# Branch sums and the first norm's bias added by accumulating transfers

## The chip, the cores and the metric

The kernel runs on one core of one Trainium2 chip. Five engines work beside each other, each through its own list of instructions in order: TensorE (PE, with its weight loads PEld), VectorE (DVE), ScalarE (ACT), GpSimd (POOL) and SyncE (SP). They wait for each other through semaphores. Transfers are issued from SP's queue or from GpSimd's and are carried out by 16 DMA engines that the queues share. The metric is the time of one execution in microseconds of device time; less is better.

## What is computed

One layer of a hybrid decoder on 256 tokens of width 2048, all in float32. What the change touches are the merging of three mixer branches and the first norm:

```python
gates = jax.nn.sigmoid(gate_logits.reshape(bsz, seq, N_BRANCH, D_MODEL) + b_gate)
merged = (gates[:, :, 0] * (y_lru @ w_branch[0])
          + gates[:, :, 1] * (y_gla @ w_branch[1])
          + gates[:, :, 2] * (y_dn @ w_branch[2]))
return merged @ w_out
...
x = _layernorm(DEEPNORM_ALPHA * x + m, ln1_g[l], ln1_b[l])
h = _squared_relu_mlp(x, mlp_w1[l], mlp_b1[l], mlp_w2[l], mlp_b2[l])
x = _layernorm(DEEPNORM_ALPHA * x + h, ln2_g[l], ln2_b[l])
```

The norm is `(xf - mu) * rsqrt(var + eps) * g + b`.

## The kernel before

**Jobs.** The kernel is a row of jobs. Each job has 1 MB of weights (`raw`, three buffers), loaded on SP's queue. ScalarE copies them to a rounded high part `hi` (line 93) and VectorE subtracts that to get the low part `lo` (line 94), eight blocks of 128x128 at a time, with three buffers for each; then TensorE multiplies with three products (high by high, low by high, high by low). The function `run_jobs` loads and splits the weights of the next job ahead of the matmuls of this one.

**Side work.** What is not part of a job is written as Python generators in the list `live`. After each job, `pump` steps them; `yield None` ends a generator's turn until the next job has been written. So a step behind `yield None` stands in TensorE's list one job later.

**The branch sums.** For each branch b (0 to 2) and each block cb of 512 columns (0 to 3), four jobs give the gate logits (`accG`), which become `gate` tiles, and two jobs give the branch's projection (`accY`). `evac_branch` then takes each of the two token halves tt: VectorE forms the product (line 907); for b = 0 it is written to the sum `mg`, for b = 1 and 2 it is written over the gate tile `t` and GpSimd adds it to `mg` (line 908). When the last branch is added, `gen_merged` is put on the list: its first step allocates and yields None, its second has TensorE transpose `mg` in 128x128 pieces into `p_m` (line 922), one job later. The gate tiles come from a pool of eight buffers (`t2`).

**The first norm.** After the output projection the tiles `xt[tt, i]` (four of 128x1024) hold the first norm's input. The MLP is fed from a normalized copy. For the second residual, `gen_res` multiplies `xt` by the row g (line 1143), adds the row b (line 1145), then scales by alpha and adds the MLP's second bias (line 1150). It runs during the first MLP jobs (`accB`, 5.6 us each). The rows are loaded on GpSimd's queue, broadcast to 128 partitions, by `row` (line 1135); each row is two tiles of 128x1024 and each tile a transfer of 512 KB.

Of the kernel before, what the change touches and what calls it, by code (L numbers as in the profile page):

```python
# [11 lines left out]
ALU = mybir.AluOpType  # L12

P = 128
# [50 lines left out]
def trunk_kernel(ctx, tc, xw, xtok, par, lat, con, wab, wa2, wB, wV, wR, wZ, wG, wBr, wO, w1, w2, rows, bg, out):  # L65
    nc = tc.nc
    ve, sc, te, gp = nc.vector, nc.scalar, nc.tensor, nc.gpsimd
# [15 lines left out]
    def b4_tile(name, shape, dt=F32):  # L83
        return b4.tile(shape, dt, tag="b4", name=name)
# [4 lines left out]
    def t1_tile(name, shape, dt=F32):  # L89
        return sm.tile(shape, dt, tag="t1", name=name, bufs=7)  # L90
# [807 lines left out]
    def evac_branch(b, cb):  # L898
        def f(tt, acc):
            if b == 0 and cb % 2 == 0:  # L900
                mg[tt, cb // 2] = b4_tile(f"mg{tt}", [P, 1024])
            m = mg[tt, cb // 2][:, (cb % 2) * 512:(cb % 2) * 512 + 512]
            t = gates.pop(tt)
            if b == 0:
                ve.scalar_tensor_tensor(m, t, 1.0, acc, ALU.add, ALU.mult)
                return
            ve.scalar_tensor_tensor(t, t, 1.0, acc, ALU.add, ALU.mult)
            gp.tensor_tensor(m, m, t, ALU.add)
            if b == 2 and tt == NT - 1:
                live.append(gen_merged(cb))  # L910
        return f

    def gen_merged(cb):
        mh.append(b4_tile(f"mh{cb}", [P, 4, T], F32R))
        ml.append(b4_tile(f"ml{cb}", [P, 4, T], F32R))
        yield None
        for kp in range(2):
            p = mx_tile("p_m")
            for a in range(2):
                c = (cb % 2) * 512 + (2 * kp + a) * P  # L920
                for tt in range(NT):
                    te.transpose(p[:, a * T + tt * P:a * T + (tt + 1) * P], mg[tt, cb // 2][:, c:c + P], ident)
            pv = p.rearrange("p (a t) -> p a t", a=2)
            hi, lo = mh[cb][:, 2 * kp:2 * kp + 2, :], ml[cb][:, 2 * kp:2 * kp + 2, :]
            sc.copy(hi, pv)
            ve.tensor_tensor(lo, pv, hi.bitcast(F32), ALU.subtract)
            yield (.7, .7)


    xt = {}  # L930
# [163 lines left out]
    for q in range(4):  # L1094
# [6 lines left out]
        for kp in range(2):  # L1101
# [6 lines left out]
            for a in range(2):  # L1108
                k = 4 * q + 2 * kp + a
                t = t1_tile("x1t", [P, T])  # L1110
# [20 lines left out]
    def row(i, nm):  # L1131
        t = []
        for j in range(2):
            r = b4_tile(f"{nm}{j}", [P, 1024])
            nc.gpsimd.dma_start(r, rows[i:i + 1, j * 1024:(j + 1) * 1024].to_broadcast([P, 1024]))
            t.append(r)
        return t

    def gen_res():
        g, b = row(0, "r_g1"), row(1, "r_b1")  # L1140
        for tt in range(NT):
            for i in range(2):
                ve.tensor_tensor(xt[tt, i], xt[tt, i], g[i], ALU.mult)
                yield (1.1, 0)
                ve.tensor_tensor(xt[tt, i], xt[tt, i], b[i], ALU.add)
                yield (1.1, 0)
        b2 = row(2, "r_b2")
        for tt in range(NT):
            for i in range(2):
                ve.scalar_tensor_tensor(xt[tt, i], xt[tt, i], ALPHA, b2[i], ALU.mult, ALU.add)  # L1150
                yield (1.1, 0)

    live.append(gen_res())


# [204 lines left out]
```

## Time and profile before

| | us |
|---|---|
| median of 3 runs | 1700.43 (lowest 1698.84) |
| the profiled execution | 1700.21, its span 1698.4 |
| TensorE busy | 1675.7 (99%) |
| VectorE busy | 1107.6 (65%) |
| ScalarE busy | 852.9 (50%) |
| GpSimd busy | 75.8 (4%) |
| DMA, all queues | 322.52 MB, mean 190 GB/s |

A timeline row gives start and duration in us, then engine, line, operation, the tile written and the tiles read, how many instructions are merged into the row, and in brackets the idle time of the engine just before and what ended it. Matmul ends are modelled: a matmul of 512 columns is drawn 0.39 us long, but the next one starts 0.23 us after it. The trace numbers lines as the listing above.

### The profile page before, as it was taken

How to read it: one execution, taken by the hardware profiler on the slowest of the kernel's cores; microseconds unless marked ns; L12 is line 12 of the kernel's file. 1: busy time of each engine (PE TensorE's matmuls, PEld its weight loads, DVE VectorE, ACT ScalarE, POOL GpSimd, SP SyncE). 2: the span in 40 equal slices, each digit the busy share in tenths (PEclk: the TensorE clock that was granted, in tenths of full speed). 3: DMA queues.
4: the chain of work that ended last, by engine and by line, in shares of the span. 5: the costliest groups of instructions: out<-in, count | busy, mean ns of one | idle time of the engine just before them, and what ended most of it. 6: DMA issues, size and time to landing. Idle time of an engine off the chain costs nothing.

```text
span 1698.4 us, 21498 instructions
## 1 busy us (share of the span) xinstructions
PE 1675.7 (99%) x8414; PEld 1416.8 (83%) x8414; DVE 1107.6 (65%) x1479; ACT 852.9 (50%) x1127; POOL 75.8 (4%) x94
## 2 busy tenths in 40 slices
PE   8999999999999999999999999999999999999997
PEld 7888887888888887888888788888888888888885
DVE  7877457788775596665556687555555555565556
ACT  6776445797444443444444454444444444444442
POOL 0000000000220203010010000000000000000000
PEclk9999999999999999999999999999999999999999
DMA  8445554444564556455565826555555555555553
GB/s 315 155 176 186 188 198 147 149 174 173 190 220 155 163 197 192 148 194 198 207 230 194 322 101 234 177 196 187 185 199 177 195 195 187 190 209 199 196 188 112
DMA packets 50774, 322.52 MB, mean 190 GB/s; under 512 B 6560, under 2 KB 6944, under 8 KB 14192
## 3 DMA queue, kind: packets, MB, share of 16 engines
q1 hardware_dynamic: 47696, 314.30, 52.4%
q0 software_dynamic: 2976, 6.84, 1.5%
q8 instruction: 66, 1.08, 0.3%
q14 instruction: 36, 0.29, 0.1%
HBM read 318.22 MB, written 2.88 MB: 189 GB/s over the span
## 4 chain that ended last, share of the span: by engine, by line
PE 97%; ACT 1%; DVE 1%; DMA 0%; issue 0%; SPq 0%; DVEq 0%
PE accB L131 22%; PE accB L133 12%; PE accM L1218 7%; PE accM L1219 7%; PE accM L1217 7%; PE accG L479 5%; PE accG L480 5%; PE accG L478 5%; PE accY L479 3%; PE accY L478 3%; PE accY L480 3%; PE accO L954 2%; PE accO L955 2%; PE accO L953 2%; PE acc L201 1%; PE accZ L478 1%
## 5 line engine op out<-in xcount | busy, mean ns | idle before, releaser
L94 DVE TENSOR_TENSOR lo<-raw,hi 128x1024 fp32r<-128x1024 f32 (+2 forms) x582 | 703.1, 1211 | 510.8 <-ACT hi L93 497.4
L93 ACT CAST hi<-raw 128x1024 fp32r<-128x1024 f32 (+2 forms) x582 | 601.7, 1037 | 735.0 <-PE accB L131 225.0
L131 PE MATMUL accB<-xx,hi 128*128 128x512 f32 x1696 | 427.5, 394 | 1.8 <-ACT hi L93 1.8
L131 PEld LDWEIGHTS accB<-xx,hi 128*128 128x128 f32 x1696 | 305.9, 189 | 58.9 <-ACT hi L93 1.9
L133 PEld LDWEIGHTS accB<-xx,lo 128*128 128x128 f32 x1696 | 232.1, 191 | 17.0 <-DVE lo L94 0.4
L133 PE MATMUL accB<-xx,lo 128*128 128x256 f32 x1696 | 237.2, 283 | 0.0
L1217 PE MATMUL accM<-hi,hh 128*128 128x512 f32 x488 | 189.8, 389 | 0.0
L1218 PE MATMUL accM<-hi,hl 128*128 128x512 f32 x488 | 189.8, 389 | 0.0
L1219 PE MATMUL accM<-lo,hh 128*128 128x512 f32 x488 | 189.8, 389 | 0.0
L478 PE MATMUL accG<-hi,xx 128*128 128x512 f32 x384 | 150.9, 393 | 0.0
L479 PE MATMUL accG<-hi,xx 128*128 128x512 f32 x384 | 149.9, 390 | 0.0
L480 PE MATMUL accG<-lo,xx 128*128 128x512 f32 x384 | 149.8, 390 | 0.0
L1217 PEld LDWEIGHTS accM<-hi,hh 128*128 128x128 f32 x488 | 91.6, 188 | 19.1
L1218 PEld LDWEIGHTS accM<-hi,hl 128*128 128x128 f32 x488 | 91.6, 188 | 19.0
L1219 PEld LDWEIGHTS accM<-lo,hh 128*128 128x128 f32 x488 | 91.6, 188 | 18.9
L480 PEld LDWEIGHTS accG<-lo,xx 128*128 128x128 f32 x384 | 72.1, 188 | 15.1
L479 PEld LDWEIGHTS accG<-hi,xx 128*128 128x128 f32 x384 | 72.1, 188 | 14.5
L478 PEld LDWEIGHTS accG<-hi,xx 128*128 128x128 f32 x384 | 72.1, 188 | 14.4
L478 PE MATMUL accY<-hi,yh 128*128 128x512 f32 x192 | 74.9, 390 | 0.0
L479 PE MATMUL accY<-hi,yl 128*128 128x512 f32 x192 | 74.7, 389 | 0.0
L480 PE MATMUL accY<-lo,yh 128*128 128x512 f32 x192 | 74.7, 389 | 0.0
L953 PE MATMUL accO<-hi,mh 128*128 128x512 f32 x128 | 49.9, 390 | 0.0
(322 smaller groups left out, 1758.4 us busy)
## 6 DMA issues: line engine op xcount, KB each, us to landing
raw<-in_w_dram SPq DMA_DIRECT2D x128, 1024.0 KB, 4.7
raw<-in_wG_dram SPq DMA_DIRECT2D x48, 1024.0 KB, 4.8
raw<-in_wB_dram SPq DMA_DIRECT2D x45, 1024.0 KB, 4.7
raw<-in_wBr_dram SPq DMA_DIRECT2D x24, 1024.0 KB, 4.8
raw<-in_wO_dram SPq DMA_DIRECT2D x16, 1024.0 KB, 4.8
raw<-in_wV_dram SPq DMA_DIRECT2D x8, 1024.0 KB, 4.7
raw<-in_wR_dram SPq DMA_DIRECT2D x8, 1024.0 KB, 4.7
raw<-in_wZ_dram SPq DMA_DIRECT2D x8, 1024.0 KB, 4.8
```

The lines of the kernel that those rows point to most:

```text
L93: i1 = sc.copy(hi, raw)
L94: i2 = ve.tensor_tensor(lo, raw, hi.bitcast(F32), ALU.subtract)
L131: te.matmul(acc, lhsT=hi[:, k, :], rhs=flat(r[:, k]), start=start and k == 0, stop=False)
L133: te.matmul(acc[:, :T], lhsT=lo[:, k, :], rhs=r[:, k, 0, :], start=False, stop=stop and k == 7)
L478: te.matmul(accs[tt], lhsT=sh, rhs=hi, start=k == 0, stop=False)
L479: te.matmul(accs[tt], lhsT=sl, rhs=hi, start=False, stop=False)
L480: te.matmul(accs[tt], lhsT=sh, rhs=lo, start=False, stop=k == 4 * nkg - 1)
L953: te.matmul(t, lhsT=sh, rhs=hi, start=k == 0, stop=False)
L954: te.matmul(t, lhsT=sl, rhs=hi, start=False, stop=False)
L1217: te.matmul(t, lhsT=sh, rhs=hi, start=k == 0, stop=False)
L1218: te.matmul(t, lhsT=sl, rhs=hi, start=False, stop=False)
L1219: te.matmul(t, lhsT=sh, rhs=lo, start=False, stop=k == NK2 - 1 and b % 512 == 0)
```

## The change

In `evac_branch` the GpSimd addition becomes a transfer that reads the product `t` and accumulates it into `mg`. In `gen_res` the row b is no longer loaded to two tiles, and the four VectorE additions become four transfers that read the row in DRAM, broadcast to 128 partitions, and accumulate it into `xt`; each is followed by `yield None`.

```diff
@@ -905,7 +905,7 @@
             ve.scalar_tensor_tensor(t, t, 1.0, acc, ALU.add, ALU.mult)
-            gp.tensor_tensor(m, m, t, ALU.add)
+            gp.dma_start(m, t, accum_op=ALU.add)
             if b == 2 and tt == NT - 1:
                 live.append(gen_merged(cb))
@@ -1137,13 +1137,13 @@
     def gen_res():
-        g, b = row(0, "r_g1"), row(1, "r_b1")
+        g = row(0, "r_g1")
         for tt in range(NT):
             for i in range(2):
                 ve.tensor_tensor(xt[tt, i], xt[tt, i], g[i], ALU.mult)
                 yield (1.1, 0)
-                ve.tensor_tensor(xt[tt, i], xt[tt, i], b[i], ALU.add)
-                yield (1.1, 0)
+                gp.dma_start(xt[tt, i], rows[1:2, i * 1024:(i + 1) * 1024].to_broadcast([P, 1024]), accum_op=ALU.add)
+                yield None
         b2 = row(2, "r_b2")
```

TensorE's list is the same; what changes there are waits. This is the first of the four places where a block of the merged sum is transposed (`mg` is the sum, a number for each token half, `p_m` the PSUM tile; a semaphore named Pool counts GpSimd's instructions, DMASW counts transfers of its queue):

```order
 L480 MATMUL accG<-lo,xx_75 128x512
-L922 MATMUL p_m<-ct,mg_4031 128x128 [waits PE_49,Pool_49]
-L922 MATMUL p_m<-ct,mg_4033 128x128 [waits Pool_49]
+L922 MATMUL p_m<-ct,mg_4031 128x128 [waits DMASW0_49,PE_49]
+L922 MATMUL p_m<-ct,mg_4033 128x128 [waits DMASW1_49]
 L922 MATMUL p_m<-ct,mg_4031 128x128
 L922 MATMUL p_m<-ct,mg_4033 128x128
```

The two transposes that read a token half first now wait for that half's transfer instead of GpSimd's addition; the other three places change in the same way.

This is the end of GpSimd's list, where the rows of the norms are loaded and the four tiles `xt_7360` to `xt_7367` get their bias (`r_b` stands for the tiles of the MLP's second bias, and before the change also of the norm's):

```order
 L1135 DMA r_g_8264<-in_rows_dram 128x1024
 L1135 DMA r_g_8266<-in_rows_dram 128x1024
-L1135 DMA r_b_8268<-in_rows_dram 128x1024
-L1135 DMA r_b_8270<-in_rows_dram 128x1024
-L1135 DMA r_b_8469<-in_rows_dram 128x1024
-L1135 DMA r_b_8471<-in_rows_dram 128x1024
...
+L1145 DMA xt_7360<-in_rows_dram 128x1024
+L1145 DMA xt_7362<-in_rows_dram 128x1024
+L1145 DMA xt_7365<-in_rows_dram 128x1024
+L1135 DMA r_b_8465<-in_rows_dram 128x1024
+L1145 DMA xt_7367<-in_rows_dram 128x1024
+L1135 DMA r_b_8467<-in_rows_dram 128x1024
```

The two loads of the MLP's second bias now stand behind the third and the fourth accumulating transfer, each of which waits for VectorE's product on its tile.

This is VectorE's list at the same place, of the changed kernel, from the second product to the last line 1150:

```order
L1143 TENSOR_TENSOR xt_7362<-xt_7362,r_g_8266 128x1024
L94 TENSOR_TENSOR lo<-raw,hi 128x1024
L1143 TENSOR_TENSOR xt_7365<-xt_7365,r_g_8264 128x1024
L1064 TENSOR_TENSOR hr<-accB,hr 128x256
L94 TENSOR_TENSOR lo<-raw,hi 128x1024
...
L1143 TENSOR_TENSOR xt_7367<-xt_7367,r_g_8266 128x1024
...
L1150 SCALAR_TENSOR_TENSOR xt_7360<-xt_7360,r_b_8465 128x1024
...
L1150 SCALAR_TENSOR_TENSOR xt_7362<-xt_7362,r_b_8467 128x1024
L1150 SCALAR_TENSOR_TENSOR xt_7365<-xt_7365,r_b_8465 128x1024
...
L1150 SCALAR_TENSOR_TENSOR xt_7367<-xt_7367,r_b_8467 128x1024
```

The four additions of line 1145 are gone from it, the products have moved closer together, and each line 1150 now waits for a transfer into its own tile as well as for the bias.

## Rows read from the trace of the kernel before

**Rows 1.** Busy part of the page: engine, us (share of the span) x instructions

```profile
PE 1675.7 (99%) x8414; PEld 1416.8 (83%) x8414; DVE 1107.6 (65%) x1479; ACT 852.9 (50%) x1127; POOL 75.8 (4%) x94
```

**Rows 2.** Chain that ended last, share of the span by engine

```profile
PE 97%; ACT 1%; DVE 1%; DMA 0%; issue 0%; SPq 0%; DVEq 0%
```

**Rows 3.** Waits of TensorE, all but the shortest: total us, times, longest us

```profile
PE acc L201 <- ACT hi L93: 4.9, 2, 4.2
PE p_x L1106 <- issue: 2.1, 1, 2.1
PE accB L131 <- ACT hi L93: 1.8, 1, 1.8
PE p_i L759 <- DVE q L752: 1.0, 1, 1.0
PE p_x L1106 <- DVE xt L1098: 0.6, 1, 0.6
```

**Rows 4.** Line 908: durations ns (min/median/max), first and last start us

```profile
L908 POOL TENSOR_TENSOR mg<-mg,gate x16: 1262/1298/2410, 636.8 to 886.5; 128x512 f32<-128x512 f32 x16
```

**Rows 5.** Timeline of 850 to 860 us, the rows of the merged sum

```profile
850.84 1.37 DVE L907 SCALAR_TENSOR_TENSOR gate<-gate,accY 128x512 f32<-128x512 f32 x2
...
851.67 3.53 POOL L908 TENSOR_TENSOR mg<-mg,gate 128x512 f32<-128x512 f32 x2 [30.01 <-DVE gate L907]
...
856.53 1.02 PEld L922 LDWEIGHTS p_m<-ct,mg 128*128 128x128 f32 x8
```

**Rows 6.** Line 922: durations ns, first and last start us

```profile
L922 PEld LDWEIGHTS p_m<-ct,mg x32: 138/140/142, 789.5 to 890.9; 128*128 128x128 f32 x32
```

**Rows 7.** DMA issues by line: KB each, median us from issue to landing

```profile
raw<-in_wG_dram SPq DMA_DIRECT2D x48, 1024.0 KB, 4.8
...
bgrow<-in_bg_dram SPq DMA_DIRECT2D x12, 256.0 KB, 4.2
...
out_dram<-xt SPq DMA_DIRECT2D x8, 256.0 KB, 2.1
wab<-in_wab_dram SPq DMA_DIRECT2D x2, 512.0 KB, 11.7
```

**Rows 8.** The same, stretches from 1022, 1029 and 962.5 us, GpSimd's queue

```profile
r_g<-in_rows_dram POOLq DMA_DIRECT2D x1, 512.0 KB, 3.6
...
r_g<-in_rows_dram POOLq DMA_DIRECT2D x1, 512.0 KB, 4.4
...
r_b<-in_rows_dram POOLq DMA_DIRECT2D x2, 512.0 KB, 8.3
```

**Rows 9.** Stretches: each engine's busy us, PEclk (granted clock), DMA share, GB/s

```profile
970.00:980.00 10.00, 6.99 (x39) 5.18 (x39) 7.54 (x21) 5.75 (x12) 0.54 (x1) 1.00 0.52 202
...
1684.00:1698.00 14.00, 2.42 (x11) 1.69 (x9) 10.28 (x20) 0.29 (x1) 0.00 (x0) 0.76 0.35 133
```

**Rows 10.** Lines 833 and 893: durations ns, first and last start us

```profile
L833 DVE TENSOR_TENSOR vn<-p_tv,btok x4: 681/682/684, 536.0 to 694.6; 128x512 f32<-128x512 f32 x4
...
L893 DVE TENSOR_TENSOR gate<-accG,bgrow x24: 671/692/693, 432.4 to 874.2; 128x512 f32<-128x512 f32 x24
```

**Rows 11.** VectorE's groups of 1000 to 1035 us: busy us, mean ns

```profile
L1145 DVE TENSOR_TENSOR xt<-xt,r_b 128x1024 f32<-128x1024 f32 x4 | 4.9, 1216 | 0.0
```

**Rows 12.** Timeline of VectorE from 968 us, three rows

```profile
1002.34 1.22 DVE L1143 TENSOR_TENSOR xt<-xt,r_g 128x1024 f32<-128x1024 f32 x1
...
1005.39 1.22 DVE L1143 TENSOR_TENSOR xt<-xt,r_g 128x1024 f32<-128x1024 f32 x1
...
1011.01 2.35 DVE L94 TENSOR_TENSOR lo<-raw,hi 128x1024 fp32r<-128x1024 f32 x2
```

**Rows 13.** Timeline of TensorE of 1009 to 1024 us, two rows

```profile
1016.84 2.00 PE L131 MATMUL accB<-xx,hi 128*128 128x512 f32 x8
1018.68 1.12 PE L133 MATMUL accB<-xx,lo 128*128 128x256 f32 x8
```

**Rows 14.** Line 1135: durations ns of an issue, first and last start us

```profile
L1135 POOL DMA_DIRECT2D r_b<-in_rows_dram x4: 537/537/538, 962.1 to 973.0; - x4
```

## The prediction

> **What bounds the kernel now.** Read the page's busy part first: TensorE is busy for 1675.7 of 1698.4 us, VectorE for two thirds of that, GpSimd for 75.8 us in all [rows 1]. Then the chain that ended last: 97% of it is TensorE [rows 2]. Then what TensorE waited for: the longest entries are 4.9 us at the start (`acc`) and a few around the first norm (`p_x`); neither `p_m` (line 922) nor any wait for GpSimd is in the list [rows 3]. So TensorE runs its list in order with hardly a gap, and an engine beside it matters only where TensorE has to stop for it. An edit that takes work from GpSimd and VectorE has little to give; the question is whether what replaces it makes TensorE stop.
>
> **The branch sums (line 908).** Removed are 16 GpSimd additions of 1.3 to 2.4 us [rows 4]. In the four places where a sum is complete, the rows show what hides them [rows 5]: VectorE writes both gate products (line 907) from 850.84 to 852.21, GpSimd adds them from 851.67 to 855.20, and TensorE starts the transposes (line 922) at 856.53, after one whole job of other matmuls. The additions end 1.3 us before TensorE comes to them. They cost nothing now, so removing them gives nothing.
>
> Added are 16 transfers of 256 KB that read two operands and write one. Eight of them (the second branch, b = 1) have the whole third branch's matmuls until anything reads the sum. Eight (b = 2) sit in four pairs, each one job ahead of its transposes, and TensorE's wait at line 922 is now on the two transfers. The time that the second transfer of a pair has: its product is ready at 852.21; GpSimd starts 0.14 us after a product is ready (850.84 + 0.69 = 851.53, start 851.67); so it is issued at 852.35. The transposes take turns between the two token halves, eight in 1.02 us, so the second sum is wanted at 856.53 + 0.13 = 856.66. That leaves 4.3 us from issue to landing. The other three places have the same spacing: the transposes' first and last starts are 789.5 and 890.9 [rows 6].
>
> No accumulating transfer is in the trace, so its landing is bounded by the nearest rows. From below: a 256 KB load in the same stage, beside the weight stream, but on SP's queue and with one operand, 4.2 us; a quiet 256 KB store 2.1 us [rows 7]. From GpSimd's own queue: 512 KB, as much as one such addition reads, landed in 3.6 us when it stood alone, in 4.4 us right after another, and in 8.3 us as the second of a pair [rows 8]. A pair of additions reads as much as that pair and writes half of it; a weight load of 1 MB, landing in 4.8 us [rows 7], goes on beside it in either case. I take the middle of 3.6 and 8.3 us, 5.9 us. TensorE then stops for 5.9 - 4.3 = 1.6 us at each of four places: 6.4 us. The bounds are 0 (anything that lands within 4.3 us) and 4 x (8.3 - 4.3) = 16 us. Nothing gives such a stop back: TensorE has no slack later in the run, its list is the same, and the engines that feed it only get further ahead. It costs no clock either: in the stretch 970 to 980 us TensorE was busy for 7.0 of 10 us and was granted 1.00; a mean of 0.76 shows only in the tail, with 2.4 of 14 us busy [rows 9].
>
> A rule speaks against this price. The Trainium skill, "DMA: Bandwidth & Descriptors", section "Anatomy of one DMA — SWDGE (gpsimd) path", fits a GpSimd-issued transfer at 2.0 us plus bytes over 436 GB/s. By it 256 KB land in an estimated 2.6 us and the sum would be 0. By the same fit 512 KB take an estimated 3.2 us; the trace has 3.6 us for one alone and 8.3 us in a pair [rows 8], so the fit holds here only without a neighbour, and the pairs of line 908 have one.
>
> The gate product is now held until its transfer has landed. Its buffer is one of eight that rotate; the next writers named in the order are line 833, last at 694.6 us, for the pair issued at 636 us, and line 893, at the next column block, some 33 us later (30.01 us of idle time and 3.53 us of additions) [rows 4, 5, 10]. Against any landing above that is free.
>
> **The norm's bias (line 1145).** Removed: four VectorE additions of 1.22 us, 4.9 us [rows 11], and two row loads. VectorE is full from 1002 to 1030 us but works ahead of TensorE: the low part that it finishes at 1011.01 + 2.35 = 1013.36 is first used at 1018.68, 5.3 us later [rows 12, 13]. So the 4.9 us are off the path too: no gain.
>
> Added: four transfers of 512 KB on GpSimd's queue, and in that queue the first load of the next bias stands behind the third of them, the second load behind the fourth. VectorE's line 1150 now waits for both. Working it through with VectorE's steps of 1.13 us (start to start) for a 128x1024 operation and 0.34 us for a 128x256 one: the second product starts at 1005.39 [rows 12], the third ends about 1008.8, so the first load is issued about 1009.5 (each issue takes 0.54 us [rows 14]); the fourth product ends about 1012.2 and the second load is issued about 1012.8. With 3.6 to 8.3 us they land at 1013.1 to 1017.8 and 1016.4 to 1021.1. VectorE comes to the two readers at about 1015.8 and 1018.3, so it stands still for 0 to 2.0 and 0 to 2.8 us, less than the 4.9 us taken from it and the 5.3 us of lead. Behind line 1150 stand the low parts (line 94) that TensorE wants, so more than about 10 us of standing still would reach it. Cost: 0, as long as the lead covers it.
>
> **The sum.** The profiled execution took 1700.2 us (span 1698.4 and 1.8 us around it), 0.2 us under the median shown. 1700.2 + 6.4 + 0 + 0.2 = 1706.8 us against that median.
>
> **The rivals.** (A) The transfers land within 4.3 us and are hidden: 1700 us, no change. For it: 3.6 and 4.2 us stand in the trace for as many or more bytes [rows 7, 8]. Against: those rows read one operand and have no twin issued half a microsecond before. The fit of "DMA: Bandwidth & Descriptors" in the Trainium skill, named above, is this case.
>
> (B) The forecast: stops of 0.5 to 4.4 us, 1702 to 1718 us.
>
> (C) The queue behind the bias becomes the wait: if an addition costs twice a load of its size, the four of them take about 4 x 8.3 = 33 us of the queue from 1003.6 on, the last reader waits until about 1037 instead of 1019, 18 us, of which some 10 are covered; TensorE loses 8 to 10 us there, and the branch sums are at their bound of 16: about 1726 us. For it: two operands are read. Against: the queue's service in a pair is nearer 4 us a load than 8.
>
> (D) Slower by over 2%: one mechanism at line 922, additions whose rows are done one after the other (read, add, write back, with the round trip exposed), so that a pair lands after 12.8 us or more. From there four stops of 8.5 us are 34 us: 1734 us and up. For it: no row shows this kind of transfer. Against: the longest median landing of any transfer on the page of 512 KB or less, in the rush at the start, is 11.7 us [rows 7].
>
> (E) Faster by over 2%: TensorE would have to lose 34 us of work, and its list is unchanged.
>
> **How the numbers follow.** B 0.50, A 0.25, C 0.15, D 0.09, E 0.01. The predicted time is B's, 1706.8. The range of 1698 to 1722 us holds A, B and about a third of C: 0.80; B alone is 1702 to 1718. About 2% (34 us) is what a measurement of this kernel can tell from no change: faster 0.01 (E), the same 0.90 (A, B, C), slower 0.09 (D).
>
> **What would show it.** TensorE's waits get a new entry, `p_m` L922 for the transfers of line 908, four times, about 1.6 us each; none, and A is right; over 8 us each, and D is. The transfer table gives the landing of `mg`: above 4.3 us it must stop TensorE. VectorE's wait at line 1150 should be short and TensorE should not wait for `lo` between 1005 and 1035 us; if it does, C is right. The prediction is wrong if additions land much faster or slower than a load on the same queue, or if the weight stream slows so much beside them that ScalarE's line 93 waits for `raw`.

## The result, and the profile after

The changed kernel took 1713.57 us (median of 6 runs, 1711.49 to 1721.35) and the kernel before, beside it, 1699.62 us: a ratio of 1.0097, 95% interval 1.0072 to 1.0122. One of the six runs of the kernel before took 2090.27 us and is left out of the ratio, which compares means and is worth 16.5 us (12.2 to 20.7). By the medians the loss is 14 us where 6.4 were forecast; it is within 2% and inside the forecast range. The profiled execution of after took 1711.49 us, its span is 1709.7 us: 11.3 us more than before.

The page of after, the rows that answer to [rows 1] and [rows 2], with the row of GpSimd's queue between them (packets, MB, share of the 16 DMA engines' span):

```profile
PE 1680.1 (98%) x8414; PEld 1418.5 (83%) x8414; DVE 1097.4 (64%) x1475; ACT 853.1 (50%) x1127; POOL 65.5 (4%) x96
...
q0 software_dynamic: 5568, 12.09, 3.3%
...
PE 79%; issue 14%; DVE 3%; DMA 2%; ACT 1%; POOL 1%; SPq 0%; POOLq 0%; DVEq 0%
```

VectorE and GpSimd are busy for 10 us less each, and the kernel is slower. The chain changes its colour, but 14% "issue" is not 14% of loss: it is followed back from an end through whichever engine released the last wait, and TensorE was still busy for 98%. The sizes stand in the waits of TensorE (total us, times, longest us), which answer to [rows 3]:

```profile
PE p_m L922 <- DMA mg<-gate: 5.2, 8, 1.0
...
PE accB L133 <- DVE lo L94: 2.5, 2, 2.3
```

These two are new: TensorE waits for the transfers of line 908, twice in each of the four places, and for a low part `lo` while the norm's bias is being added.

**Where the first loss sits.** The first of the four places in the timeline of after, in the form of [rows 5], with the idle time of an engine in brackets:

```profile
782.64 1.37 DVE L907 SCALAR_TENSOR_TENSOR gate<-gate,accY 128x512 f32<-128x512 f32 x2
...
783.62 1.75 POOL L908 DMA_DIRECT2D mg<-gate  x2 [30.89 <-DVE gate L907]
...
789.07 0.14 PEld L922 LDWEIGHTS p_m<-ct,mg 128*128 128x128 f32 x1 [0.77 <-PE accG L480]
...
790.29 0.75 PEld L922 LDWEIGHTS p_m<-ct,mg 128*128 128x128 f32 x7 [1.08 <-DMA mg<-gate]
```

TensorE was ready at 789.07 - 0.77 = 788.30. It starts the first transpose when the first half has landed and stops again after one, until the second half has. The last seven end at 791.04; without a stop all eight would have ended at 788.30 + 1.02 = 789.32 [rows 5]. So 1.7 us are lost here. Line 922 of after tells the sum over the four places, by its first and last start:

```profile
L922 PEld LDWEIGHTS p_m<-ct,mg x32: 138/140/142, 789.1 to 896.7; 128*128 128x128 f32 x32
```

Before, the first transpose started at 789.5 and the last at 890.9 [rows 6]. Now TensorE is ready for the first at 788.3, some 1.1 us earlier, and starts the last at 896.7, 5.8 us later: 6.9 us are lost on the way. The list of waits has only 5.2, because the end of a matmul is modelled late; the weight loads' idle time (0.77 + 1.08 at this place) is nearer to the loss.

**Where the second loss sits.** DMA issues (KB each, median us from issue to landing), and GpSimd's list from 1010 us:

```profile
mg<-gate POOLq DMA_DIRECT2D x16, 256.0 KB, 5.4
...
xt<-in_rows_dram POOLq DMA_DIRECT2D x4, 512.0 KB, 9.9
...
r_b<-in_rows_dram POOLq DMA_DIRECT2D x2, 512.0 KB, 14.2
```

```profile
1010.88 0.88 POOL L1145 DMA_DIRECT2D xt<-in_rows_dram  x1 [47.30 <-ACT hr L1063]
1013.94 0.88 POOL L1145 DMA_DIRECT2D xt<-in_rows_dram  x1 [2.18 <-DVE xt L1143]
1015.87 0.85 POOL L1145 DMA_DIRECT2D xt<-in_rows_dram  x1 [1.05 <-DVE xt L1143]
1016.41 0.87 POOL L1135 DMA_DIRECT2D r_b<-in_rows_dram  x1
```

The first tile of the next bias, `r_b`, is issued at 1016.41 behind three accumulating transfers and takes 14.2 us, to 1030.6. What VectorE does with that, answering to [rows 12], and TensorE, answering to [rows 13]:

```profile
1022.21 0.42 DVE L1064 TENSOR_TENSOR hr<-accB,hr 128x256 f32<-128x256 f32 x1
1030.70 1.23 DVE L1150 SCALAR_TENSOR_TENSOR xt<-xt,r_b 128x1024 f32<-128x1024 f32 x1 [8.07 <-DMA r_b<-in_rows_dram]
...
1032.18 1.22 DVE L94 TENSOR_TENSOR lo<-raw,hi 128x1024 fp32r<-128x1024 f32 x1
1034.35 2.36 DVE L1150 SCALAR_TENSOR_TENSOR xt<-xt,r_b 128x1024 f32<-128x1024 f32 x2 [0.94 <-DMA r_b<-in_rows_dram]
```

```profile
1026.32 2.00 PE L131 MATMUL accB<-xx,hi 128*128 128x512 f32 x8
...
1029.12 2.00 PE L131 MATMUL accB<-xx,hi 128*128 128x512 f32 x8
1033.45 1.86 PE L133 MATMUL accB<-xx,lo 128*128 128x256 f32 x8 [2.33 <-DVE lo L94]
1035.12 2.95 PE L131 MATMUL accB<-xx,hi 128*128 128x512 f32 x8
...
1039.28 2.00 PE L131 MATMUL accB<-xx,hi 128*128 128x512 f32 x8
```

VectorE stands for 8 us at line 1150. Behind it in its list is the `lo` that TensorE wants, so TensorE stops too. Then it is slow: eight matmuls of line 133 take 1.86 us instead of 1.12 [rows 13], eight of line 131 2.95 instead of 2.00. The stretches of this place (length, PE, PEld, DVE, ACT and POOL busy, then granted clock, DMA share, GB/s) show why:

```profile
1028.00:1031.00 3.00, 3.00 (x18) 2.40 (x16) 0.30 (x1) 0.00 (x0) 0.00 (x0) 1.00 1.07 259
1031.00:1033.40 2.40, 0.12 (x1) 0.00 (x0) 2.40 (x3) 1.10 (x2) 0.00 (x0) 1.00 1.01 398
1033.40:1035.10 1.70, 1.65 (x8) 1.65 (x9) 0.75 (x1) 1.70 (x4) 0.00 (x0) 0.60 0.59 140
1035.10:1036.50 1.40, 1.40 (x6) 1.11 (x5) 1.40 (x2) 1.40 (x3) 0.00 (x0) 0.50 0.88 363
```

Just behind the stop the granted clock falls to 0.50, that is to 1.2 GHz and not 2.4: finer stretches have 0.50 from about 1033.8 to 1037.1 (0.60 is the mean of both levels) and 1.00 again from 1037.3. From 1029.12 to 1039.28 TensorE did two rounds of lines 131 and 133; the round ahead of them, undisturbed, took 1029.12 - 1026.32 = 2.80 us. 10.16 us instead of 5.6: 4.6 us are lost, 2.5 by the stop and 2.1 behind it. There a second wait for `lo` takes 0.15 us, and 3.4 us at half the clock cost an estimated 1.7. At line 922, with shorter stops (0.38 and 0.89 us on TensorE's own rows), the clock stayed at 1.00.

**The sum of after.** Span 1698.4 - 1.1 (everything up to 782 us is that much earlier) + 6.9 (four places of line 922) + 4.6 (bias) + 0.9 (first norm, below) = 1709.7 us. The change's own part is 6.9 + 4.6 = 11.5 us; the 1.1 and the 0.9 are differences between two executions that no run ties to the change (in the profiles with the transposes at their old place TensorE is ready for the first anywhere from 785.3 to 789.5 us).

### The profile page after: what moved, and what is told of

It is laid out like the page before. It is cut to its first block, busy times and chain, and to the rows that moved or that the text cites. A ratio compares the mean times of both kernels' runs of the same rounds, so it can differ in the third digit from the quotient of the medians.

```text
span 1709.7 us, 21510 instructions
## 1 busy us (share of the span) xinstructions
PE 1680.1 (98%) x8414; PEld 1418.5 (83%) x8414; DVE 1097.4 (64%) x1475; ACT 853.1 (50%) x1127; POOL 65.5 (4%) x96
## 3 DMA queue, kind: packets, MB, share of 16 engines
q8 instruction: 66, 1.08, 0.3%
## 4 chain that ended last, share of the span: by engine, by line
PE 79%; issue 14%; DVE 3%; DMA 2%; ACT 1%; POOL 1%; SPq 0%; POOLq 0%; DVEq 0%
PE accB L131 22%; PE accB L133 11%; PE accM L1218 7%; PE accM L1219 7%; PE accM L1217 7%; PE accG L479 2%; PE accG L480 2%; PE accG L478 2%; PE accO L954 2%; PE accO L955 2%; PE accO L953 2%; PE acc L201 1%; DVE lo L94 1%; PE accZ L478 1%; PE accV L478 1%
```

## The experiments

All ratios are against the kernel before, run on the same chip; they compare means, so they can differ a little from the quotient of the medians.

| kernel | ratio, 95% interval | median us (before) |
|---|---|---|
| e1_sums | 1.0060, 1.0047 to 1.0073 | 1709.60 (1699.17) |
| e2_bias | 1.0023, 1.0014 to 1.0032 | 1702.73 (1699.17) |
| e3_sums_later | 1.0001, 0.9993 to 1.0010 | 1699.66 (1699.17) |
| e4_bias_first | 1.0007, 0.9999 to 1.0016 | 1701.30 (1699.17) |
| e5_both | 1.0016, 1.0007 to 1.0024 | 1701.56 (1698.76) |
| e6_sums_copy | 1.0027, 1.0015 to 1.0039 | 1703.54 (1698.76) |
| e7_bias_copy | 1.0006, 0.9996 to 1.0016 | 1700.13 (1698.76) |
| e8_one_half | 1.0013, 1.0004 to 1.0023 | 1700.98 (1698.76) |
| e9_no_adds | 0.9993, 0.9984 to 1.0002 | 1697.37 (1699.35) |

### e1_sums: only the branch sums

```diff
-            gp.tensor_tensor(m, m, t, ALU.add)
+            gp.dma_start(m, t, accum_op=ALU.add)
```

> Only the branch sums (line 908) accumulate by transfer; the norm's bias is added by VectorE as before. Theory (two separate costs: four stops at line 922 of about 1.75 us, and a queue behind the bias): the four stops stay, 7.0 us in all, and nothing is lost between 1000 and 1040 us, so 7 us above the kernel before, ratio 1.004. Rival 1 (the bias alone makes the loss, the stops at line 922 are caught up later): same time as before, ratio 1.000. Rival 2 (the parts share one cause, the load on the DMA engines): most of the 14 us remains, ratio 1.006 or more.

The median is 10.4 us above before (8.0 to 12.4 by the interval). The waits of TensorE, and the landing of the 16 transfers:

```profile
PE p_m L922 <- DMA mg<-gate: 6.7, 8, 1.2
```

```profile
mg<-gate POOLq DMA_DIRECT2D x16, 256.0 KB, 5.9
```

The mechanism is the forecast one, and no wait for `lo` is there. Its size varies: the pairs landed in 5.7 to 6.4 us here and in 5.6 to 5.7 in the profile of after, and by the starts of the weight loads the four places lost 8.3 us in this execution, against the 6.9 of after. So most of the 14 us comes from line 908. The ratio is that of Rival 2 and above the theory's 1.004; the sum of the parts (e2_bias) and e3_sums_later speak against a shared cause.

### e2_bias: only the norm's bias

```diff
-        g, b = row(0, "r_g1"), row(1, "r_b1")
+        g = row(0, "r_g1")
...
-                ve.tensor_tensor(xt[tt, i], xt[tt, i], b[i], ALU.add)
-                yield (1.1, 0)
+                gp.dma_start(xt[tt, i], rows[1:2, i * 1024:(i + 1) * 1024].to_broadcast([P, 1024]), accum_op=ALU.add)
+                yield None
```

> Only the norm's bias accumulates by transfer; the branch sums stay on GpSimd. Theory: the two loads of the MLP's second bias land some 14 us after issue behind the accumulating transfers, VectorE stands about 8 us at line 1150, TensorE stops about 2.3 us for lo and then runs some us at half the granted clock: 4.6 us in the profiled execution, up to 7 in others, ratio 1.003 to 1.004. Rival 1 (the bias is covered as predicted): ratio 1.000. Rival 2 (one shared cause): the two parts alone add up to clearly less than both together.

The median is 3.6 us above before; the ratio of 1.0023 (up to 1.0032) is a little under the expected 1.003 to 1.004. The stop of after comes back without the branch sums; the wait of TensorE and the stretch after it:

```profile
PE accB L133 <- DVE lo L94: 2.6, 2, 2.5
```

```profile
1024.00:1026.00 2.00, 0.45 (x2) 0.02 (x1) 1.84 (x3) 0.24 (x1) 0.00 (x0) 1.00 0.99 352
...
1028.00:1030.00 2.00, 2.00 (x8) 1.71 (x8) 2.00 (x2) 1.95 (x3) 0.00 (x0) 0.50 0.79 297
```

The clock falls to 0.50 behind the stop here as well. The two parts add up: 10.4 + 3.6 = 14.0 us, the whole change by its medians. By the ratios it is 14.1 us, within the 12.2 to 20.7 of the whole.

### e3_sums_later: the transposes one job later

```diff
-            gp.tensor_tensor(m, m, t, ALU.add)
+            gp.dma_start(m, t, accum_op=ALU.add)
...
         ml.append(b4_tile(f"ml{cb}", [P, 4, T], F32R))
         yield None
+        yield None
         for kp in range(2):
```

> Branch sums by transfer, bias as before, and one more empty step in gen_merged, so that TensorE's transposes stand one job (5.4 us) later in its list. Theory: the second transfer of a pair lands 5.6 us after issue, the transposes now come about 9.7 us after it, so all four waits of p_m for mg go and the time is that of the kernel before, ratio 1.000. Rival (what costs is not the wait but the traffic beside the weight stream): the ratio stays at that of the branch sums alone, about 1.004.

No `p_m` is left in TensorE's waits (one weight load stood for 0.4 us), the time is that of before (1.0001, 0.9993 to 1.0010), and the transfers land as slowly as ever:

```profile
mg<-gate POOLq DMA_DIRECT2D x16, 256.0 KB, 5.9
```

So the loss of e1_sums was the wait, and the traffic itself cost nothing that can be measured. Nor is there a gain: the additions taken from GpSimd were worth nothing.

### e4_bias_first: the next bias loaded ahead of the transfers

```diff
         g = row(0, "r_g1")
+        b2 = row(2, "r_b2")
...
-        b2 = row(2, "r_b2")
```

This stands on top of the edit of e2_bias.

> Bias by transfer, branch sums on GpSimd, and the row loads of the MLP's second bias written ahead of the four accumulating transfers in GpSimd's list. Theory: they land before VectorE needs them, line 1150 then waits only for its own tile's transfer (at most 1 to 3 us each, inside TensorE's lead of 5 us), TensorE does not wait for lo, ratio 1.000. Rival (the DMA engines are full from 1010 us on, so the accumulating transfers themselves come too late, or the weights do): VectorE still stands 5 us or more at line 1150 or ScalarE waits for raw, ratio 1.002 or more.

The ratio is 1.0007, 0.9999 to 1.0016. `r_b` lands in 7.7 us instead of 14.3, and what line 1150 waits for is now its own accumulating transfer (4.8 us at the longest, where 1 to 3 were expected). TensorE still waits for `lo`, which the theory excluded, but for less, and the clock in the stretch with the stop stays up:

```profile
PE accB L133 <- DVE lo L94: 1.4, 1, 1.4
```

```profile
1026.00:1029.00 3.00, 1.55 (x11) 1.13 (x10) 3.00 (x5) 0.89 (x1) 0.54 (x1) 1.00 0.79 283
```

By the ratios about two thirds of the loss of e2_bias, 0.0016 of 0.0023, were the place of two loads in a queue; each ratio is known to about 0.0009, so the share is rough.

### e5_both: the whole change with both moves

```diff
         yield None
+        yield None
         for kp in range(2):
...
         g = row(0, "r_g1")
+        b2 = row(2, "r_b2")
...
-        b2 = row(2, "r_b2")
```

This stands on top of the whole change.

> The whole change with two moves of order: the transposes of the merged block stand one job later in TensorE's list (as in e3_sums_later), and the second bias is loaded right behind g, ahead of the accumulating transfers (as in e4_bias_first). Theory: the two losses are two waits for a landing, independent of each other, and each move takes its own away. Then the time is that of e4_bias_first and e3_sums_later together: ratio 1.000 to 1.002, 1699 to 1702.5 us, no p_m in TensorE's waits, one wait for lo of about 1.4 us at most, granted clock 1.00 at 1022 to 1034 us. Rival: the added traffic costs time by itself (for instance it slows the weight stream), so the sum of the parts shows again although the waits are gone: ratio above 1.003, over 1705 us.

The ratio is 1.0016 (1.0007 to 1.0024), inside what the theory gave; TensorE waits for no `p_m`, and for 1.4 us for `lo`. Of the 14 us, 2.8 are left, close to what e4_bias_first may have (2.1 by its median, up to 2.7 by its interval), and there is no gain. No arrangement tried beats the kernel before.

### e6_sums_copy: the same transfers without the accumulation

```diff
-            gp.tensor_tensor(m, m, t, ALU.add)
+            gp.dma_start(m, t)
```

> Only line 908 differs from the kernel before: the transfer overwrites the sum with the gate product and accumulates nothing, so the addition of the three branches is left out; the norm's bias is added by VectorE as before. The bytes read from the gate tile and written to mg are the same, the accumulation is gone. Theory: the accumulation (a second operand read) sets the landing. Then a plain transfer of 256 KB at the same place lands in at most 4.3 us (median), its issue takes about 0.54 us and not 0.87, TensorE waits for p_m by under 0.3 us a place, and the time is within 1 us of the kernel before (ratio 0.999 to 1.001). Rival: the landing is set by the twin transfer and the weight stream beside it; then it stays at 5.4 to 5.9 us, TensorE's wait stays at 1 us and over for each of the four places, ratio 1.004 to 1.007.

Line 908 and the time from its transfers to their landing, then TensorE's wait:

```profile
L908 POOL DMA_DIRECT2D mg<-gate x16: 546/548/607, 634.0 to 885.1; - x16
...
DMA to landing us min/median/max: 2.3/5.0/6.2
```

```profile
PE p_m L922 <- DMA mg<-gate: 2.4, 6, 1.3
```

Neither expectation holds alone. The issue falls to 0.55 us as the theory said, but the landing only to 5.0 us, and 4.8 us of the 10.4 remain. The accumulation is about half of it, by a longer issue and a longer landing. The rest is there with a plain pair too; what part of that is the twin transfer and what part the weight stream beside it, this run does not separate. GpSimd's queue tells what the accumulation costs the DMA engines, here of before (first), e1_sums and e6_sums_copy:

```profile
q0 software_dynamic: 2976, 6.84, 1.5%
```

```profile
q0 software_dynamic: 5280, 11.04, 2.8%
```

```profile
q0 software_dynamic: 4256, 11.04, 2.1%
```

The bytes counted in the last two are the same. The shares are of spans of 1698.4, 1707.3 and 1700.7 us, so the 16 transfers added 22.3 us against 10.2, or 1.4 us against 0.6 us of all 16 engines for each. The Trainium skill, "Collectives: The Full Stack", section "The bandwidth ceiling: the fold count and why AG ≠ RS ≠ AR", says of a ReduceScatter between cores that its add needs two source reads, and that it passes about half of what a copying AllGather does. The ratio of 2.2 here, within one core (the shares are rounded, so 1.9 to 2.6), is near that factor.

### e7_bias_copy: the bias without the accumulation

```diff
-        g, b = row(0, "r_g1"), row(1, "r_b1")
+        g = row(0, "r_g1")
...
-                ve.tensor_tensor(xt[tt, i], xt[tt, i], b[i], ALU.add)
-                yield (1.1, 0)
+                gp.dma_start(xt[tt, i], rows[1:2, i * 1024:(i + 1) * 1024].to_broadcast([P, 1024]))
+                yield None
```

> Only the norm's bias differs from the kernel before: four transfers in the changed kernel's places, but plain, so that each overwrites its xt tile with the bias row; the product with g and the addition are lost from the result. The branch sums are on GpSimd as before. Theory: the accumulation makes the queue at 1010 to 1030 us twice as long as six plain row loads would make it. Then the first bias tile of line 1150 (r_b) lands in 7 to 9 us and not 14, the DMA share over 1015 to 1030 us falls below 0.9, VectorE stands less than 4 us at line 1150, TensorE waits for lo by under 1 us with granted clock 1.00, and the time is that of the kernel before (ratio 0.999 to 1.001). Rival: it is the six transfers of 512 KB close together and not the accumulation; then r_b lands in 12 us or more and the ratio is about 1.002 as in e2_bias.

```profile
r_b<-in_rows_dram POOLq DMA_DIRECT2D x2, 512.0 KB, 9.1
```

```profile
PE accB L133 <- DVE lo L94: 0.3, 1, 0.3
```

The landing falls from 14.3 to 9.1 us, the wait from 2.6 to 0.3 us, and the time to that of before. Two points missed: VectorE stands 1.8 + 3.2 = 5.0 us at line 1150 and not less than 4, and the DMA share stays full, as the stretches from 1015 us of e7_bias_copy show beside those of before (second fence):

```profile
1015.00:1020.00 5.00, 5.00 (x32) 4.41 (x31) 3.17 (x5) 1.81 (x3) 0.00 (x0) 1.00 1.03 425
1020.00:1025.00 5.00, 5.00 (x31) 4.42 (x30) 1.80 (x3) 2.88 (x4) 0.00 (x0) 1.00 0.99 370
1025.00:1030.00 5.00, 4.68 (x26) 3.74 (x25) 5.00 (x7) 1.82 (x3) 1.08 (x2) 1.00 0.44 144
```

```profile
1015.00:1020.00 5.00, 5.00 (x31) 4.46 (x30) 5.00 (x7) 2.17 (x3) 0.00 (x0) 1.00 0.59 206
```

Transfers of 512 KB close together fill the engines either way, but the plain ones are done by 1025 us. With the accumulation, in e2_bias, the same share moves fewer bytes (277 and 315 GB/s where it was 425 and 370) and lasts longer:

```profile
1015.00:1020.00 5.00, 5.00 (x31) 4.46 (x30) 0.96 (x2) 1.05 (x1) 0.00 (x0) 1.00 1.03 277
1020.00:1025.00 5.00, 4.45 (x24) 3.48 (x22) 0.84 (x1) 0.00 (x0) 0.00 (x0) 1.00 1.04 315
1025.00:1030.00 5.00, 3.09 (x12) 2.80 (x13) 4.06 (x5) 4.19 (x6) 0.00 (x0) 0.72 0.81 297
```

### e8_one_half: one transfer instead of a pair

```diff
-            gp.tensor_tensor(m, m, t, ALU.add)
+            if tt == NT - 1:
+                gp.dma_start(m, t, accum_op=ALU.add)
+            else:
+                gp.tensor_tensor(m, m, t, ALU.add)
```

> Only line 908 differs from the kernel before, and only for the second token half: its sum is added by an accumulating transfer, the first half's by GpSimd. The norm's bias is as before. Theory: the landing of 5.4 to 5.9 us comes from two such transfers side by side; one alone lands in 3.3 to 4.5 us, so TensorE waits for p_m by at most 0.5 us at each place, 0 to 2 us in all, ratio 1.000 to 1.0015. Rival: one transfer takes as long alone (5 us and more, by its two operands beside the weight stream); then the second half's transposes wait about 1 us and more at each place, and the ratio is 1.003 to 1.006.

The eight transfers, then TensorE's wait (the edit moves line 922 to 925):

```profile
DMA to landing us min/median/max: 3.4/4.1/6.8
```

```profile
PE p_m L925 <- DMA mg<-gate: 2.7, 1, 2.7
```

At three places a single one lands in 4.0 to 4.2 us; no matmul waits, and the weight loads stand for 0.27 to 0.46 us. So without its twin even an accumulating transfer all but makes the deadline, as the theory said. At the last place it took 6.8 us, and that one stop of 2.7 us is about the 2.2 us by which the median is longer. Why it was slow there is open; the weight load was issued 2.0 us ahead of it, as at the third place, but took 7.5 us to land and not 4.7 to 5.0 as at the other three.

The stop of 2.7 us is longer than those of after and e2_bias, and yet the granted clock stays at 1.00:

```profile
888.00:890.00 2.00, 0.13 (x1) 0.13 (x2) 1.15 (x1) 0.00 (x0) 0.00 (x0) 1.00 0.96 385
890.00:892.00 2.00, 2.00 (x13) 1.78 (x14) 0.93 (x2) 1.07 (x2) 0.00 (x0) 1.00 0.30 123
```

### e9_no_adds: what the removed work was worth

```diff
-            gp.tensor_tensor(m, m, t, ALU.add)
...
-        g, b = row(0, "r_g1"), row(1, "r_b1")
+        g = row(0, "r_g1")
...
-                yield (1.1, 0)
-                ve.tensor_tensor(xt[tt, i], xt[tt, i], b[i], ALU.add)
```

> The kernel before with the additions taken out and nothing in their place: GpSimd's line 908 is gone (the second and third branch's products are formed and not added), VectorE's four additions of line 1145 and the two loads of their row are gone (the norm's bias is left out of the second residual). It measures what the removed work costs. Theory: nothing, since TensorE is the bound and the work is hidden; ratio 0.999 to 1.001, 1697 to 1700.5 us, TensorE's waits as in the kernel before. Rival: the removed work was partly on the path (through GpSimd and VectorE slowing each other, or through the wait for lo), so a gain is hidden under the losses that the other runs show; ratio below 0.998, under 1696 us.

The ratio is 0.9993, 0.9984 to 1.0002: with nothing in their place, the additions save at most 2.7 us and not measurably any. There was next to nothing to win.

## Why the prediction was right, and where it was not

**No gain from the removed work: right.** e9_no_adds shows it directly.

**Line 908: right in the mechanism, too small in the term.** At the first place the forecast's steps can be set beside the timeline. It had the second transfer issued 1.51 us after the pair of products starts; it was 783.62 + 0.88 - 782.64 = 1.86 us. It had the second half wanted 5.82 us after that start; it was 788.30 + 0.14 - 782.64 = 5.80. It had a landing of 5.9 us; it was 790.29 - 784.50 = 5.8. So the landing was forecast well, but with luck: it was the middle of two bounds, with no row of this kind of transfer. And 8.3 was misread: in [rows 8] it is the median of the pair, whose first landed in 7.9 and whose second in 8.8 us; with 8.8 the same steps give 6.2 us and a cost of 7.6. (The load of 4.4 us did not stand right behind another either; nothing rests on it.) What was missed is that issuing an accumulating transfer takes GpSimd 0.87 us and not 0.54 as a row load does [rows 14], and the second stands behind the first. Forecast 1.6 us a place, measured 1.7 in this execution; 6.4 against 6.9 in all. By medians the term is larger: 10.4 us in e1_sums, with its interval from 8.0 to 12.4. The profiled execution of after was the lowest of its six, and that of e1_sums lost 8.3 us at this line, so the wait varies from execution to execution.

**The fit that spoke against the price.** The Trainium skill, "DMA: Bandwidth & Descriptors", section "Anatomy of one DMA — SWDGE (gpsimd) path", gave an estimated 2.6 us for 256 KB. A plain one landed in 5.0 us at the median, an accumulating pair in 5.4 to 5.9, a single one in 4.1; the lowest landing of any was 2.3 us. So the trace disagrees here, and the measurements decide.

**The norm's bias at 0: wrong.** The forecast had VectorE standing 0 to 2.0 us at the first line 1150, covered by its lead. VectorE came there at 1030.70 - 8.07 = 1022.6 and `r_b` was issued at 1016.4. Both are within 0.2 us of the forecast's 1015.8 and 1009.5 once the 6.7 us by which this execution was behind there (-1.1 + 6.9 + 0.9) are taken off. What failed is the landing: 3.6 to 8.3 us was taken for a load behind accumulating transfers, from plain loads in a pair [rows 8], and it was 14.2 us. e7_bias_copy names the accumulation as the cause (9.1 us without it), and e4_bias_first the place in the queue (7.7 us ahead of it). This is rival C's mechanism, at half of its price: 4.6 us in the profile, 3.6 us by e2_bias, where 8 to 10 us were worked out, because the queue took 23 us, from the first issue at 1010.9 to the second `r_b` at 1034.3 (the second line 1150 starts at 1034.35), and not 33.

**"It costs no clock": wrong at one place.** It was read from [rows 9], one stretch of one execution. At line 922 it held. Behind the 2.3 us stop for `lo` the clock fell to 0.50, and an estimated 1.7 of the 4.6 us come from that. The length of a stop does not decide it alone: behind the 2.7 us of e8_one_half the clock stayed at 1.00. What does is open. Nor was the row itself steady: the stretch of the first norm, with a stop of 2.1 us, has 1.00 in [rows 9] and in e9_no_adds, but in the other nine profiles a lower clock, as in e7_bias_copy, which changes nothing ahead of that stretch, and in after, where it is the 0.9 us of the sum. So the runs do not show that the change causes those 0.9 us. Here is e7_bias_copy, then after:

```profile
970.00:980.00 10.00, 7.24 (x36) 6.07 (x35) 7.49 (x21) 6.48 (x13) 0.00 (x0) 0.83 0.01 2
```

```profile
980.00:985.00 5.00, 3.53 (x18) 3.15 (x19) 3.59 (x11) 4.60 (x9) 0.00 (x0) 0.75 0.01 3
985.00:990.00 5.00, 5.00 (x29) 4.40 (x28) 5.00 (x13) 4.97 (x11) 0.00 (x0) 0.91 0.01 2
```

**The sum.** Forecast 1706.8, measured 1713.57: 10.4 and 3.6 where 6.4 and 0 stood. The time even lies in B's own 1702 to 1718, because B allowed stops of up to 4.4 us a place; that is partly luck, since 3.6 of the 14 us came from C's mechanism, which the forecast had priced at 0. The step that failed is the landing of a load behind accumulating transfers: 14.2 us and not 3.6 to 8.3.

## What to carry to other kernels

Before moving work from an idle engine to a transfer, ask whether the work is on the path at all; here it was not, and the transfer's landing then stood where an addition of 1.3 us had stood. A consumer that comes one job after its producer has a deadline in microseconds: compare it with the issue of the first of two transfers plus the landing of the second, and put the consumer one job later if it does not fit. Loads that something needs soon belong ahead of slow transfers in the queue, not behind them.

## What the runs showed of the hardware

- An accumulating transfer of 256 KB from SBUF to SBUF took GpSimd 0.84 to 1.15 us to issue, against 0.55 to 0.61 for the plain one, and about 1.4 us of all 16 DMA engines against 0.6.
- An accumulating transfer of 512 KB from a broadcast row in DRAM landed in 5.0 to 13.5 us in after, with four of them issued within 9 us; a plain load behind three of them took 14.2 us.
- A stop of TensorE of 2.3 to 2.5 us was followed by a granted clock of 0.50 for some 3.4 us, in after and in e2_bias; after stops of 1.4 us (e4_bias_first) and of 2.7 us (e8_one_half) it stayed at 1.00; the stop of 2.1 us at the first norm was followed by 1.00 in two profiles and by a lower clock in the other nine, of nearly the same program.
